# One block of gMLP, SSD and PEER experts on one core: gather rates by stage, and three one-hots made by one comparison

## Chip, cores and metric

The kernel runs on one NeuronCore of a Trainium2 chip. The metric is the device time of one execution in microseconds (us); less is better. Times of the runs of one kernel are given by their median.

## What is computed

The reference is one block over 1024 tokens of width 1024, in fp32. A gMLP branch and an SSD branch (a chunked state-space scan with a causal convolution) are gated, merged, projected and normalised to `x1`. Then comes PEER: 8 heads pick 16 of 16384 experts for every token, that is 128 experts a token.

```python
...
    s1 = jnp.einsum('thd,hkd->thk', q[:, :, 0], sub_k1).astype(jnp.float32)
    s2 = jnp.einsum('thd,hkd->thk', q[:, :, 1], sub_k2).astype(jnp.float32)
    v1, i1 = lax.top_k(s1, PEER_TOPK)
    v2, i2 = lax.top_k(s2, PEER_TOPK)
    cand = (v1[..., :, None] + v2[..., None, :]).reshape(T, PEER_HEADS, PEER_TOPK * PEER_TOPK)
...
    gates = jax.nn.softmax(best, axis=-1)
...
        u = u_tab[eb]
        act = jax.nn.gelu(jnp.einsum('tkd,td->tk', u, xb).astype(jnp.float32))
        return jnp.einsum('tk,tkd->td', (gb * act).astype(x.dtype), v_tab[eb])
...
```

The block's output is the layer norm of `ALPHA * x1`, the PEER sum and a gated projection of `p`.

## The kernel before

**Groups.** The tokens are worked on in three groups (GROUPS): two blocks of 128, three blocks, three blocks. `front(gi)` runs a group through its stages: the gmlp stage (gates of the branch, its mixing and output product), the SSD stage, the merge (`ya`, lines 538 to 551), the query stage (w_o, normalisation, w_q, top 16, and `ple`), and for the last group the gates stage and the dense stage. Products in fp32 are made of three passes over rounded halves (`mm3`, lines 155 to 157); each weight is split into `whi` (line 149, ScalarE) and `wlo` (line 150, VectorE).

**Two ways for the experts.** For the first two groups (5 blocks) the expert rows are gathered. `experts_u` gathers a row of the u table for each of 128 experts of 128 tokens (line 837, an indirect DMA of 128 rows of 4 KB, issued by GpSimd) and multiplies it with `x1` on VectorE with a running sum (line 856). `experts_v` gathers rows of the v table, four at a time, and adds them up on TensorE with diagonal weights (line 898, tile `pacc`): 8 products in the program for a group of four rows, 16 records in the profile. In all these are 5 x 256 = 1280 gathers. The rows go through a ring of 12 buffers.

For the last group the experts are computed densely. `dense_scores` makes the products of all tokens with a part of the u table ahead and stores them in DRAM (`s`). `dense_gates` makes, token by token, a 128x128 matrix of gates as a product of two one-hot matrices: `o1` compares a row of numbers 0 to 127 (`iota`) with the first half of the expert's number, `o2` with the second, times the gate. Four tokens share a PSUM tile. Of these four, the first `o1` is made by ScalarE (lines 974 and 975), the other three by VectorE (line 977); all four `o2` by VectorE (line 979); line 981 multiplies. `dense` then runs through the 16384 experts in 16 steps: products with the u table (or a load of `s`), times the gates, and products with the v table into `po`.

**The order of the work.** Gathers run beside the fronts of the second and third group. Each `yield` of `front` names a cost; a gather costs 1.47. After each yield the loop at the end of `block_kernel` lets as many gathers follow as the cost times `SIDE[phase[0]]` pays for. `phase[0]` is 0 in the gmlp stage, 1 in SSD stage and merge, 2 in the query stage, 3 in the gates stage, 4 in the dense stage. What is left after the last front runs alone. The scheduler keeps that order but for the priorities that are written into the code.

Of the kernel before, what the change touches and what calls it, by code (L numbers as in the profile page):

```python
# [8 lines left out]
F32 = mybir.dt.float32  # L9
# [4 lines left out]
AF = mybir.ActivationFunctionType  # L14
OP = mybir.AluOpType
# [9 lines left out]
TC, GI = 32, 4  # L25
# [3 lines left out]
TOPK = 16  # L29
OFF = [sum(TOPK // (a + 1) for a in range(n)) for n in range(TOPK + 1)]  # L30
PAIRS = HEADS * TOPK
O1_ACT = 1
LAG = 6
QLAG = 4
TOGETHER = 2000
# [7 lines left out]
AHEAD_G = 40  # L43
LEAD = 50
UNIT = 5.35
SIDE = (0.82, 0.78, 0.80, 0.66, 0.78)
ALPHA = 2 ** 0.25
EPS = 1e-5

# [32 lines left out]
def block_kernel(ctx, tc, a, out):  # L82
    nc = tc.nc
    V, A, PE, DMA, POOL = nc.vector, nc.scalar, nc.tensor, nc.sync, nc.gpsimd
# [112 lines left out]
    ps, ps_es, phase, tk_, selects = {}, [None], [0], [None], []  # L197
# [20 lines left out]
    def front(gi):  # L218
# [24 lines left out]
        with tc.tile_pool(name="ga", bufs=1, side=side_) as ga, \  # L243
# [75 lines left out]
            for g4 in range(0, 8, 4):  # L319
# [3 lines left out]
                for g in range(g4, g4 + 4):  # L323
                    V.scalar_tensor_tensor(add[:, g], pr[:, g - g4], gmb[:, g:g + 1], add[:, g],
                                           op0=OP.mult, op1=OP.add)
# [11 lines left out]
            for g in range(8):  # L337
# [4 lines left out]
                for c in range(NB):  # L342
# [5 lines left out]
                                       op0=OP.mult, op1=OP.add)  # L348
# [29 lines left out]
        with tc.tile_pool(name="sa", bufs=1, side=side_) as sa, tc.tile_pool(name="sb", bufs=2, side=side_) as sb:  # L378
# [141 lines left out]
            for n in range(3):  # L520
                pgs.append(channel_major(a["w_g"][8 + n], xh, xl))
                yield unit
                c = next(tail, None)
# [5 lines left out]
            V.reciprocal(rrow, rrow)  # L529


        mp_es = ExitStack()
        mp = mp_es.enter_context(tc.tile_pool(name="mp", bufs=1, side=other))
        mh = mp.tile([128, 8, T], F32R, name="mh")
# [117 lines left out]
        tk_es.close()  # L652
        phase[0] = 3
        yield from merge((take(ahead, AHEAD[1]), AHEAD[1] * unit), (dense_gates(gi, NB, pst), 38 * NB))
        yield from ahead
        phase[0] = 4
# [297 lines left out]
    def dense_gates(gi, NB, pst):  # L954
        with tc.tile_pool(name="da", bufs=1) as da, tc.tile_pool(name="db", bufs=3) as db:
            iota = da.tile([128, 128], F32, name="iota")
            POOL.iota(iota, pattern=[[1, 128]], base=0, channel_multiplier=0,
                      allow_small_or_imprecise_dtypes=True)
            T = NB * 128
            sT = da.tile([128, 3, T], F32, name="sT")  # L960
            for c in range(NB):
                DMA.dma_start(sT[:, :, c * 128:c * 128 + 128], sel_t[gi, c])

            g_d[gi] = dram.tile([T // TC, 128, 128 * TC], F32, name=f"g_{gi}")
            for c in range(T // TC):
                gt = db.tile([128, 128, TC], F32, name="gt", bufs=2)
                for n4 in range(0, TC, 4):
                    p = pst.tile([128, 4, 128], F32, name="mt", tag="mt")
                    for i in range(4):
                        n = c * TC + n4 + i  # L970
                        o1 = db.tile([128, 128], F32, name="o1")
                        if i < O1_ACT:

                            A.activation(o1, iota, AF.Abs, scale=-1.0, bias=sT[:, 0, n:n + 1])
                            A.activation(o1, o1, AF.Relu, scale=-1.0, bias=1.0)
                        else:
                            V.tensor_scalar(o1, iota, sT[:, 0, n:n + 1], None, op0=OP.is_equal)
                        o2 = db.tile([128, 128], F32, name="o2")
                        V.tensor_scalar(o2, iota, sT[:, 1, n:n + 1], sT[:, 2, n:n + 1],  # L979
                                        op0=OP.is_equal, op1=OP.mult)  # L980
                        PE.matmul(p[:, i, :], lhsT=o1, rhs=o2, start=True, stop=True)  # L981
                    A.copy(gt[:, :, n4:n4 + 4].rearrange("p i t -> p t i"), p)
                    yield 1.2
                gf = gt.rearrange("p i t -> p (i t)")
                for b in range(0, 128 * TC, 2048):
                    DMA.dma_start(g_d[gi][c, :, b:b + 2048], gf[:, b:b + 2048])
# [76 lines left out]
    for gi in range(NG):  # L1063
        owed = 0.0
        for cost in front(gi):
            owed += cost * SIDE[phase[0]]
            if not gate_t:
                owed = 0.0
            while side and owed > 0:
                step = next(side[0], None)  # L1070
                if step is None:
                    side.pop(0)
                else:
                    owed -= step
        if GROUPS[gi][1] == "gather":
            selects += [select(gi, c) for c in range(GROUPS[gi][0])]
            side += [experts([(gi, c, r0 + c * 128) for c in range(GROUPS[gi][0])])]
        r0 += GROUPS[gi][0] * 128
# [79 lines left out]
```

## Time and profile before

| | before |
|---|---|
| median of 3 runs | 3757.99 us (3755.95 to 3758.19) |
| the profiled execution | 3754.28 us |
| its span | 3752.6 us |
| TensorE busy | 3439.9 us (92%) |
| VectorE busy | 2935.7 us (78%) |
| ScalarE busy | 1754.2 us (47%) |
| GpSimd busy | 1569.2 us (42%) |
| DMA | 1183.88 MB, mean 315 GB/s |

Busy shares are means over the whole span; the stages have different limits, so a table by stage says more. TensorE's busy time holds some waiting, since its products overlap. The stages are, in us from the span's start: first group to 497; second group 497 to 709 (gmlp), to 1067 (SSD), to 1134 (merge), to 1293 (query); third group to 1543, 1925, 1996, 2320; gates stage to 2616; dense stage 2664 to 3674; then the tail.

### The profile page before, as it was taken

The page shows a single profiled execution, that of the slowest core. Times are in us where ns is not written, and L with a number is a line of the kernel's source. Part 1 is how long each engine was busy: PE and PEld are TensorE (multiplying, and loading weights), DVE is VectorE, ACT ScalarE, POOL GpSimd, SP SyncE. Part 2 cuts the span into 40 slices and gives each one's busy share as a digit, 9 for nine tenths or more (in the row PEclk, how much of TensorE's full clock was granted, in tenths as well). Part 3 has the DMA queues.
Part 4 walks back from the last instruction along what each step waited for, and adds up shares of the span by engine and source line. Part 5 has one row for each costly group of instructions (what it writes and reads, how often), then busy time and mean ns, then how long its engine had stood idle before and what let it go on. Part 6 is the DMA issues. An engine that isn't in the chain of part 4 may idle for free. (4 is left out here: it accounts for less than half of the span.)

```text
span 3752.6 us, 59429 instructions
## 1 busy us (share of the span) xinstructions
PE 3439.9 (92%) x21390; PEld 2939.4 (78%) x21390; DVE 2935.7 (78%) x6823; ACT 1754.2 (47%) x2671; POOL 1569.2 (42%) x1310
## 2 busy tenths in 40 slices
PE   9899996999998988999987989889989999999995
PEld 8888896888887977888777878777768878778771
DVE  6677898898987989894698999997676676676652
ACT  6888443475752333475742334675333323233220
POOL 0000004744455444543455455334455455455544
PEclk9999998999999999999999999999999999999997
DMA  6444647989899787989899899899999999999987
GB/s 212 160 164 160 229 174 249 389 308 356 311 369 391 288 305 285 358 308 323 295 326 337 302 337 371 329 335 370 349 378 379 363 360 370 357 365 395 367 313 283
DMA packets 405703, 1183.88 MB, mean 315 GB/s; under 512 B 40736, under 2 KB 135968, under 8 KB 402336
## 3 DMA queue, kind: packets, MB, share of 16 engines
q0 software_dynamic: 187488, 682.71, 48.5%
q1 hardware_dynamic: 217200, 494.76, 36.8%
q8 instruction: 168, 2.75, 0.3%
q10 hardware_dynamic: 720, 2.62, 0.2%
q14 instruction: 127, 1.04, 0.1%
HBM read 1121.01 MB, written 58.92 MB: 314 GB/s over the span
## 5 line engine op out<-in xcount | busy, mean ns | idle before, releaser
L149 ACT CAST whi<-raw 128x1024 fp32r<-128x1024 f32 (+1 forms) x676 | 700.5, 1041 | 1127.2 <-PE mm L156 582.2
L837 POOL DMA_INDIRECT row<-in_peer_u_dram,idx x640 | 796.3, 1244 | 1004.3 <-PE pacc L898 376.2
L157 PE MATMUL mm<-xh,wlo 128*128 128x384 f32 (+2 forms) x3160 | 1055.3, 335 | 57.4 <-DVE wlo L150 50.5
L150 DVE TENSOR_TENSOR wlo<-raw,whi 128x1024 fp32r<-128x1024 f32 (+1 forms) x676 | 817.1, 1211 | 371.0 <-ACT whi L149 298.7
L155 PE MATMUL mm<-xh,whi 128*128 128x384 f32 (+2 forms) x3160 | 1060.6, 336 | 38.0 <-ACT whi L149 27.2
L156 PE MATMUL mm<-xl,whi 128*128 128x384 f32 (+2 forms) x3160 | 1046.8, 331 | 0.6 <-DVE xl L139 0.6
L837 POOL DMA_INDIRECT row<-in_peer_v_dram,idxT x640 | 758.9, 1186 | 681.9 <-DVE row L856 210.9
L856 DVE SCALAR_TENSOR_TENSOR row<-row,x1b 128x1024 f32<-128x1024 f32 x640 | 773.6, 1217 | 22.9 <-DMA row<-in_peer_u_dram,idx 18.5
L155 PEld LDWEIGHTS mm<-xh,whi 128*128 128x128 f32 (+1 forms) x3160 | 606.9, 192 | 93.4 <-ACT whi L149 51.5
L157 PEld LDWEIGHTS mm<-xh,wlo 128*128 128x128 f32 (+1 forms) x3160 | 606.1, 192 | 78.1 <-DVE wlo L150 60.1
L156 PEld LDWEIGHTS mm<-xl,whi 128*128 128x128 f32 (+1 forms) x3160 | 606.3, 192 | 9.5 <-issue 2.8
L898 PE MATMUL pacc<-row,zw 128*32 128x512 f32 x2560 | 321.3, 621 | 39.2 <-DMA row<-in_peer_v_dram,idxT 39.1
L155 PE MATMUL po<-whi,ewh 128*128 128x512 f32 x768 | 313.9, 409 | 20.1 <-DVE eacc L1051 17.9
L156 PE MATMUL po<-wlo,ewh 128*128 128x512 f32 x768 | 309.4, 403 | 17.1 <-DVE wlo L150 17.0
L157 PE MATMUL po<-whi,ewl 128*128 128x512 f32 x768 | 308.2, 401 | 0.0
L898 PEld LDWEIGHTS pacc<-row,zw 128*32 128x32 f32 x2560 | 68.5, 111 | 193.9 <-issue 140.6
L155 PEld LDWEIGHTS po<-whi,ewh 128*128 128x128 f32 x768 | 147.3, 192 | 86.3 <-DVE eacc L1051 19.9
L156 PEld LDWEIGHTS po<-wlo,ewh 128*128 128x128 f32 x768 | 147.5, 192 | 50.4 <-DVE wlo L150 18.5
L852 POOL DMA_DIRECT2D x1b<-x x5 | 3.0, 606 | 434.2 <-DMA x<-x 434.1
L138 ACT CAST ewh<-ew 128x384 fp32r<-128x384 f32 x128 | 65.6, 513 | 242.4 <-DVE ew L1019 175.3
L157 PEld LDWEIGHTS po<-whi,ewl 128*128 128x128 f32 x768 | 147.4, 192 | 36.1
L981 PE MATMUL mt<-o,o 128*128 128x128 f32 x768 | 148.9, 302 | 15.1 <-DVE o L979 6.0
(275 smaller groups left out, 5609.3 us busy)
## 6 DMA issues: line engine op xcount, KB each, us to landing
raw<-in_peer_uT_dram SPq DMA_DIRECT2D x128, 512.0 KB
raw<-in_peer_vd_dram SPq DMA_DIRECT2D x128, 512.0 KB
raw<-in_w_xbc_dram SPq DMA_DIRECT2D x96, 512.0 KB
raw<-in_w_g_dram SPq DMA_DIRECT2D x48, 512.0 KB
raw<-in_w_z_dram SPq DMA_DIRECT2D x48, 512.0 KB
raw<-in_ssd_w_out_dram SPq DMA_DIRECT2D x48, 512.0 KB
raw<-in_w_q_dram SPq DMA_DIRECT2D x48, 512.0 KB
g<-gt SPq DMA_DIRECT2D x24, 1024.0 KB
```

The source lines that it names most:

```text
L138: A.copy(hi, src)
L149: A.copy(hi, raw)
L150: V.tensor_sub(lo, raw, hi.bitcast(F32))
L155: PE.matmul(p, lhsT=lh, rhs=rh, start=start, stop=False, skip_group_check=skip)
L156: PE.matmul(p, lhsT=lh, rhs=rl, start=False, stop=False, skip_group_check=skip)
L157: PE.matmul(p, lhsT=ll, rhs=rh, start=False, stop=stop, skip_group_check=skip)
L837: g = POOL.indirect_dma_start(out=t, out_offset=None, in_=a[tab], in_offset=bass.IndirectOffsetOnAxis(ap=ix, axis=0))
L852: POOL.dma_start(x1, x1_d[gi, c])
L856: u = V.scalar_tensor_tensor(t, t, 1.0, x1, op0=OP.mult, op1=OP.mult, accum_out=act[:, k:k + 1])
L898: return PE.matmul(pacc[q * 32:q * 32 + 32, h * 512:h * 512 + 512], lhsT=zws[z][:, q, r % 4, :], rhs=ts[q][:, h * 512:h * 512 + 512], star ...
L981: PE.matmul(p[:, i, :], lhsT=o1, rhs=o2, start=True, stop=True)
```

## The change

The table of rates gets other values and a sixth one for the merge, which becomes phase 5. In `dense_gates` the plain one-hots of the last three of four tokens are made by one VectorE comparison of 128x384, `others`, with two buffers of its own; it compares `iota`, repeated three times, with three columns of `sT`, each repeated 128 times. The first token's one-hot stays on ScalarE, in the three buffers of `o1`.

```diff
-O1_ACT = 1
...
-SIDE = (0.82, 0.78, 0.80, 0.66, 0.78)
+SIDE = (0.70, 0.82, 0.68, 0.66, 0.86, 1.1)
...
+        phase[0] = 5
         mp_es = ExitStack()
...
                     p = pst.tile([128, 4, 128], F32, name="mt", tag="mt")
+
+                    n0 = c * TC + n4
+                    first = db.tile([128, 128], F32, name="o1")
+                    A.activation(first, iota, AF.Abs, scale=-1.0, bias=sT[:, 0, n0:n0 + 1])
+                    A.activation(first, first, AF.Relu, scale=-1.0, bias=1.0)
+                    others = db.tile([128, 3, 128], F32, name="o3", bufs=2)
+                    V.tensor_tensor(others, iota[:, None, :].to_broadcast([128, 3, 128]),
+                                    sT[:, 0, n0 + 1:n0 + 4].unsqueeze(2).to_broadcast([128, 3, 128]),
+                                    op=OP.is_equal)
                     for i in range(4):
-                        n = c * TC + n4 + i
-                        o1 = db.tile([128, 128], F32, name="o1")
-                        if i < O1_ACT:
-
-                            A.activation(o1, iota, AF.Abs, scale=-1.0, bias=sT[:, 0, n:n + 1])
-                            A.activation(o1, o1, AF.Relu, scale=-1.0, bias=1.0)
-                        else:
-                            V.tensor_scalar(o1, iota, sT[:, 0, n:n + 1], None, op0=OP.is_equal)
+                        n = n0 + i
+                        o1 = others[:, i - 1] if i else first
                         o2 = db.tile([128, 128], F32, name="o2")
                         V.tensor_scalar(o2, iota, sT[:, 1, n:n + 1], sT[:, 2, n:n + 1],
                                         op0=OP.is_equal, op1=OP.mult)
```

What the rates make of the gathers follows from the code: the sum of a stage's costs times its rate by 1.47 (with what is owed from the yield before).

| stage | sum of costs | rate | gathers | rate after | gathers after |
|---|---|---|---|---|---|
| gmlp, second group (the first yields pay nothing) | 134.8 | 0.82 | 55 | 0.70 | 47 |
| SSD, second group | 265.6 | 0.78 | 141 | 0.82 | 148 |
| merge, second group | 64.2 | 0.78 | 34 | 1.1 | 48 |
| query, second group | 146.7 | 0.80 | 80 | 0.68 | 68 |
| gmlp, third group | 134.8 | 0.82 | 76 | 0.70 | 65 |
| SSD, third group | 265.6 | 0.78 | 141 | 0.82 | 148 |
| merge, third group | 64.2 | 0.78 | 34 | 1.1 | 48 |
| query, third group | 235.0 | 0.80 | 128 | 0.68 | 109 |
| gates | 219.5 | 0.66 | 98 | 0.66 | 98 |
| dense | 849.0 | 0.78 | 451 | 0.86 | 497 |
| left | | | 42 | | 4 |

Three places of the instruction order. Line numbers of the change are one less up to line 530, the same from there to line 968, and three more behind the comparisons.

VectorE, in the merge of the third group, the first of its eight rounds; line 545 opens a round, 547 to 549 are its additions and products, `ml` (139, or 138) its low half, and `row,act` is a gathered u row. Before:

```order
L545 TENSOR_TENSOR sg<-sg,rrow 128x384
L150 TENSOR_TENSOR wlo<-raw,whi 128x1024
L547 TENSOR_TENSOR ya<-ya,mm 128x384
L856 SCALAR_TENSOR_TENSOR row,act<-row,x1b 128x1024
L548 TENSOR_TENSOR ya<-ya,sg 128x384
L856 SCALAR_TENSOR_TENSOR row,act<-row,x1b 128x1024
L549 TENSOR_TENSOR ya<-ya,m0t 128x384
L856 SCALAR_TENSOR_TENSOR row,act<-row,x1b 128x1024
L139 TENSOR_TENSOR ml<-ya,mh 128x384
L856 SCALAR_TENSOR_TENSOR row,act<-row,x1b 128x1024
```

With the change:

```order
L545 TENSOR_TENSOR sg<-sg,rrow 128x384
L547 TENSOR_TENSOR ya<-ya,mm 128x384
L149 TENSOR_TENSOR wlo<-raw,whi 128x1024
L548 TENSOR_TENSOR ya<-ya,sg 128x384
L856 SCALAR_TENSOR_TENSOR row,act<-row,x1b 128x1024
L549 TENSOR_TENSOR ya<-ya,m0t 128x384
L856 SCALAR_TENSOR_TENSOR row,act<-row,x1b 128x1024
L138 TENSOR_TENSOR ml<-ya,mh 128x384
L856 SCALAR_TENSOR_TENSOR row,act<-row,x1b 128x1024 x4
```

Six u rows stand in the round in place of four. From line 545's first row of this merge to the next stage's first row (line 577) there are 37 u rows before and 51 with the change; from there to the gates 71 before and 56 with the change. In the gmlp stages (from line 312 to the first convolution, line 392) there are 59 and 37 before, 55 and 34 with the change.

TensorE, at the end of the program; `po` is the dense stage's output, `pacc` the sum of gathered v rows, x8 a group of four. Before:

```order
L157 MATMUL po<-whi,ewl 128x512
L155 MATMUL po<-whi,ewh 128x512
L156 MATMUL po<-wlo,ewh 128x512
L157 MATMUL po<-whi,ewl 128x512
L898 MATMUL pacc<-row,zw_139 32x512 x32
L898 MATMUL pacc<-row,zw_138 32x512 x32
L898 MATMUL pacc<-row,zw_139 32x512 x32
```

With the change:

```order
L156 MATMUL po<-whi,ewl 128x512
L154 MATMUL po<-whi,ewh 128x512
L155 MATMUL po<-wlo,ewh 128x512
L156 MATMUL po<-whi,ewl 128x512
L898 MATMUL pacc<-row,zw_139 32x512 x16
```

Twelve groups stand behind the last dense product before, two with the change; the other ten have moved in among the dense products.

VectorE, in the gates stage; `o_..` are the one-hots (977 the plain ones and 979 those with the gate; 975 and 982 with the change). Before:

```order
L979 TENSOR_SCALAR o_25100<-iota,sT 128x128
L856 SCALAR_TENSOR_TENSOR row,act<-row,x1b 128x1024
L150 TENSOR_TENSOR wlo<-raw,whi 128x1024
L977 TENSOR_SCALAR o_25103<-iota,sT 128x128
L979 TENSOR_SCALAR o_25105<-iota,sT 128x128
L977 TENSOR_SCALAR o_25108<-iota,sT 128x128
L979 TENSOR_SCALAR o_25110<-iota,sT 128x128
L977 TENSOR_SCALAR o_25113<-iota,sT 128x128
L979 TENSOR_SCALAR o_25115<-iota,sT 128x128
```

With the change:

```order
L975 TENSOR_TENSOR o_25113<-iota,sT 128x384
L982 TENSOR_SCALAR o_25115<-iota,sT 128x128
L982 TENSOR_SCALAR o_25118<-iota,sT 128x128
L982 TENSOR_SCALAR o_25121<-iota,sT 128x128
L982 TENSOR_SCALAR o_25124<-iota,sT 128x128
```

Seven comparisons for four tokens have become five (between them stand rows of other work).

## Rows read from the trace of the kernel before

**Rows 1.** Table of engines by stage, the columns in its first line.

```profile
core 0: us, PE busy (x) PEld busy (x) DVE busy (x) ACT busy (x) POOL busy (x), PEclk, DMA share, GB/s
497.00:709.00 212.00, 180.26 (x1132) 172.49 (x1131) 198.07 (x506) 83.60 (x108) 87.50 (x62) 0.93 0.73 265
709.00:1067.00 358.00, 345.62 (x2272) 304.14 (x2270) 317.47 (x625) 244.32 (x392) 175.96 (x146) 0.99 0.89 331
1067.00:1134.00 67.00, 63.69 (x365) 58.27 (x366) 55.58 (x93) 23.06 (x31) 38.62 (x32) 0.97 1.00 382
1134.00:1293.00 159.00, 147.80 (x1005) 128.47 (x1005) 137.63 (x476) 50.85 (x81) 77.39 (x64) 0.97 0.91 345
1293.00:1543.00 250.00, 219.18 (x1410) 190.39 (x1413) 228.65 (x674) 93.28 (x125) 120.03 (x94) 0.94 0.84 306
1543.00:1925.00 382.00, 363.80 (x2435) 305.90 (x2427) 280.79 (x513) 245.71 (x393) 178.46 (x152) 0.99 0.88 315
1925.00:1996.00 71.00, 61.74 (x313) 58.41 (x314) 68.88 (x111) 21.08 (x29) 38.62 (x32) 0.93 0.99 368
1996.00:2320.00 324.00, 289.35 (x1862) 259.00 (x1864) 304.64 (x996) 113.21 (x154) 155.11 (x126) 0.96 0.90 330
2320.00:2616.00 296.00, 265.82 (x1643) 219.25 (x1636) 267.79 (x847) 196.57 (x345) 122.82 (x108) 0.97 0.92 343
2664.00:3674.00 1010.00, 972.77 (x4962) 762.75 (x4964) 672.85 (x1039) 306.09 (x407) 520.32 (x439) 0.98 0.97 364
```

**Rows 2.** The same table for steps inside the dense stage.

```profile
2708.00:2777.00 69.00, 69.00 (x370) 58.12 (x367) 52.46 (x84) 26.02 (x34) 42.82 (x37) 1.00 1.02 396
3359.00:3505.00 146.00, 146.00 (x781) 119.94 (x780) 102.06 (x153) 47.33 (x62) 84.19 (x69) 1.00 1.01 388
3505.00:3558.00 53.00, 47.16 (x219) 33.60 (x218) 36.60 (x56) 14.04 (x20) 27.21 (x22) 0.94 1.00 367
3631.00:3674.00 43.00, 43.00 (x221) 28.88 (x224) 16.25 (x26) 8.85 (x11) 16.34 (x17) 1.00 0.74 259
```

**Rows 3.** Timeline of the end: start, duration, engine, line, idle time before.

```profile
3641.50 1.92 PE L898 MATMUL pacc<-row,zw 128*32 128x512 f32 x16
3643.36 0.50 PE L155 MATMUL po<-whi,ewh 128*128 128x512 f32 x1
...
3672.62 0.39 PE L157 MATMUL po<-whi,ewl 128*128 128x512 f32 x1
...
3683.49 1.23 DVE L1057 TENSOR_TENSOR eacc<-eacc,row 128x1024 f32<-128x1024 f32 x1
...
3731.78 0.94 POOL L837 DMA_INDIRECT row<-in_peer_v_dram,idxT  x1 [0.31 <-issue]
...
3738.09 2.96 PE L898 MATMUL pacc<-row,zw 128*32 128x512 f32 x16 [2.44 <-DMA row<-in_peer_v_dram,idxT]
...
3741.10 1.22 DVE L802 TENSOR_TENSOR x1b<-x1b,pacc 128x1024 f32<-128x1024 f32 x1 [43.87 <-PE pacc L898]
```

**Rows 4.** The page's first line and its row of the gathers' queue.

```profile
span 3752.6 us, 59429 instructions
...
q0 software_dynamic: 187488, 682.71, 48.5%
```

**Rows 5.** Groups by line and shape: busy us, mean ns of one, idle before.

```profile
L856 DVE SCALAR_TENSOR_TENSOR row<-row,x1b 128x1024 f32<-128x1024 f32 x640 | 773.6, 1217 | 22.9 <-DMA row<-in_peer_u_dram,idx 18.5 <-issue 3.4
...
L979 DVE TENSOR_SCALAR o<-iota,sT 128x128 f32<-128x128 f32 x384 | 131.9, 358 | 0.7 <-PE mm L157 0.2 <-PE mt L981 0.2
...
L977 DVE TENSOR_SCALAR o<-iota,sT 128x128 f32<-128x128 f32 x288 | 84.2, 293 | 18.6 <-PE mt L981 10.5 <-PE mm L156 3.8 <-PE mm L155 2.1
...
L1019 DVE TENSOR_TENSOR ew<-ew,gte 128x384 f32<-128x384 f32 x128 | 71.2, 562 | 84.0 <-DMA ew<-s 66.0 <-ACT ew L1017 9.2 <-DMA gte<-g 8.4
...
L856 DVE DVE_READ_ACCUMULATOR row<-row,x1b 128x1 f32 x640 | 51.7, 81 | 0.0
...
L450 DVE TENSOR_TENSOR xdd<-mt,dtd 128x384 f32<-128x384 f32 x32 | 17.6, 549 | 3.7 <-PE mt L446 2.9 <-issue 0.8
```

## Prediction

> **What bounds the kernel now.** I read the table by stage first [rows 1]: it cuts the span at the instructions that only one stage has. The reader is to see that no engine bounds all of it. The gmlp stages (497 to 709, 1293 to 1543) and the query stage of the last group (1996 to 2320) are VectorE's: it is busy 198.07 of 212, 228.65 of 250 and 304.64 of 324 us, TensorE and the DMA engines less. The two merges (1067 to 1134, 1925 to 1996) have DMA shares of 1.00 and 0.99; in the second VectorE is full too (68.88 of 71). The SSD stages are TensorE's (345.62 of 358, 363.80 of 382) with VectorE and DMA below. In the gates stage (2320 to 2616) VectorE has 267.79 of 296, TensorE 265.82, the DMA share is 0.92. The dense stage (2664 to 3674) has TensorE at 972.77 of 1010 and a DMA share of 0.97.
>
> Inside the dense stage [rows 2] there are two kinds of step. Where the products with the u table are computed beside it, TensorE is busy all of 146 us and the DMA share is 1.01; where they are loaded (3505 to 3558), TensorE is idle for 6 of 53 us and the DMA share is 1.00. Only the last step has DMA to spare: 0.74 over 43 us.
>
> Last come the tail's instructions [rows 3]. The last product of the dense stage begins at 3672.62; 12 groups of gathered rows follow it (the order shows them), and TensorE waits for each pair of groups to land. The last gather is issued at 3731.78, its group starts at 3738.09, the closing additions at 3741.10, and the span ends at 3752.6 [rows 4].
>
> **The price of one gather.** It costs what the stage is short of. On VectorE a u row takes 1217 ns, and 81 for the accumulator [rows 5]: 1.30 us; a v row almost nothing. On TensorE four v rows take 1.86 us (from 3641.50 to 3643.36 [rows 3]), a u row nothing. On the DMA engines a gather is 0.524 MB; the gathers' queue q0 holds 48.5% of 16 engines' span for 682.71 MB [rows 4], so 0.485 x 3752.6 x 0.524 / 682.7 = 1.40 us.
>
> **The change part by part.** The numbers of gathers by stage are those of the table with the diff: cost times rate by 1.47.
>
> Gmlp stages: 8 and 11 gathers fewer. If all were u rows, VectorE would give back 10.4 and 14.3 us; the rows that the order shows on VectorE there are only some 4 fewer in each. I take -6 for each, ends 0 and -12.
>
> SSD stages: 7 gathers more each. TensorE bounds them, half are v rows: 3.5 / 4 x 1.86 = 1.6 us; I take +2 each, ends 0 and 7 x 1.40 = +10.
>
> Merges: 14 gathers more each. The first has no DMA left: 14 x 1.40 = 20 us, less what slips into the next stage; I take +15. In the second the order puts 14 more u rows on VectorE, 14 x 1.30 = 18 us, on a full engine: +18. Ends +5 and +20. What is queued behind these rows on VectorE is the merge's own additions and the weights' low halves, so TensorE waits for them.
>
> Query stages: 12 and 19 fewer. In the first, TensorE is at 147.80 of 159 and gives back v rows, VectorE u rows: -7. In the second VectorE is the bound and the order shows 15 u rows fewer: 15 x 1.30 = 19.5; I take -17. Ends 0 and -25.
>
> Gates stage: the rate stays. 288 comparisons of 128x128 at 293 ns [rows 5] become 96 of 128x384. No comparison of that form is in the trace. The nearest rows are the broadcast multiplication of two operands of 128x384 (549 ns) and the plain one (562 ns); I take 555. Upper end: three of the old ones, 879 ns, no gain. Saved on VectorE: 96 x (879 - 555) = 31 us. The four other comparisons of each four tokens stay (358 ns each), and so do ScalarE's two operations for the first token. VectorE would fall to 237 us, under the DMA engines' 0.92 x 296 = 272, which are late next. So of 31 us I take -18, ends -27 and 0.
>
> One rule speaks against this part. The Trainium skill (VectorE: DVE Perf Modes, section Mode 2×_2P — use both read ports for one tensor) has an fp32 operation with one tensor at two elements a cycle and one with two tensors at one. With that page's fixed term of about 150 cycles, an estimate from it is 223 ns for an old comparison and 556 for the new, 11 us saved instead of 31. The row's 293 ns does not agree with it: the same page's one element a cycle would be 290.
>
> Dense stage: the rate rises from 0.78 to 0.86, 451 gathers become 497. Its lower end is TensorE alone: in its order 12 groups behind the last dense product become 2, so 10 x 1.86 = 18.6 us come into the stage. Its upper end is the DMA queue alone: 46 x 0.524 MB at the stage's own 364 GB/s = 66 us. The loaded steps and the first ones are at their DMA limit, the computed pairs at both limits, the last step has room for 8 gathers. I take +40, near the middle.
>
> The Trainium skill (DMA: Bandwidth & Descriptors, section Where 436 GB/s comes from) states some 358 GB/s of HBM for one core as what binds such transfers; by it the upper end, 46 x 0.524 / 0.358 = 67 us, would be the price. The rows do not bear out that limit, 396 GB/s over 69 us and 388 over 146 [rows 2], but they leave little above.
>
> Tail: from 3673.0 to 3752.6 it is 79.6 us now. With two groups left, the last gathers are issued about when the last dense product runs. Then stand 6.3 us from issue to product (3731.78 to 3738.09), 3.0 of product and 11.5 of closing: 21 us. VectorE closes the dense blocks at the same time (until 3684.72 [rows 3]), which may push it by up to 5. I take 25, so -54; ends -50 and -58.
>
> Nothing is taken for POOL: it issues the same 1280 gathers, and in no stage is it busy over 58%.
>
> Sum: -12 + 4 + 33 - 24 - 18 + 40 - 54 = -31. The profiled execution took 3754.3 us (span 3752.6, 1.7 around it): 3723. It stands 3.7 us under the median of the runs shown, so the median I forecast is 3727, and the rivals below have the same 3.7 in them.
>
> **The rivals.**
>
> One: TensorE alone bounds the dense stage (+19), and the gates stage gives -27. For it: TensorE idles only 37 us of 1010, and windows of 396 GB/s exist. Against it: the loaded step's DMA share of 1.00. Time: 3727 - 21 - 9 = 3697.
>
> Two: the wide comparison is no cheaper than three narrow ones, or the gates stage was not VectorE's. Then -18 falls away: 3745. For it: TensorE and VectorE are 2 us apart there. Against it: the two-operand rows of the same size.
>
> The Trainium skill's rule on two operands (VectorE: DVE Perf Modes, same section) lies on this side: 11 of 31 us left makes -6 of -18, an estimate of 3739.
>
> Three: in dense stage and merges each gather pays at the stage's rate, 0.524 / 0.364 = 1.44 us: 66 and 2 x 20 instead of 40 and 33, so 3727 + 33 = 3760, no change. What the tail gave is spent before it. The limit of the Trainium skill's DMA page (DMA: Bandwidth & Descriptors, same section) would be this case.
>
> Four, slower: the DMA engines are the bound wherever their share is 0.9 or more. Then rival three's prices hold, and taking VectorE's work out of the gates stage (0.92) gives nothing, of the query stages (0.91, 0.90) only half: 3760 + 18 + 12 = 3790. It decides from the point at which the dense stage grows by over 60 us while the gates stage keeps its 296. Against it: 396 GB/s beside stages at 330 to 345.
>
> That the change does not do what it says is unlikely: the order shows the moved rows in merges and tail.
>
> **How the numbers follow.** Forecast 0.50, with a range of its own of 3710 to 3745; rival one 0.14, two 0.10, three 0.14, four 0.12. A measurement of this kernel can tell some 0.2% (7.5 us) from no change: faster 0.50 + 0.14 + 0.10 = 0.74, same 0.14, slower 0.12. The range goes from just under rival one to just over rival three, 3693 to 3764, and leaves out rival four and the outer half of rival one, under 0.2.
>
> **What would show it.** Right: a tail of 21 to 30 us behind the last dense product; the 96 comparisons at 540 to 580 ns and a gates stage of 270 to 285 us; merges of 80 to 90 us; a last query stage near 307; a dense stage of 1035 to 1060. Wrong: a dense stage over 1070, or a gates stage that keeps 296 with VectorE under 240 busy (rivals three and four); comparisons of 700 ns or more (rival two); merges that stay under 72, which would say that DMA had room.

## The result and the profile after

The changed kernel takes 3716.8 us (median of 4 runs, 3707.43 to 3720.9), the kernel before beside it 3758.09 us. The ratio is 0.9886, 95% interval 0.9869 to 0.9904: about 41 us faster, where 3727 was forecast in a range of 3693 to 3764. The profiled execution took 3720.9 us (span 3719.2), 33.4 us of span less than the one of before.

The table of engines by stage of the changed kernel, its columns as in [rows 1]; the two merges, the last query stage and the dense stage:

```profile
1079.00:1155.00 76.00, 68.71 (x393) 58.42 (x393) 61.82 (x105) 21.91 (x29) 49.12 (x40) 0.96 1.03 406
...
1939.00:2019.00 80.00, 60.35 (x289) 56.84 (x288) 76.22 (x126) 18.57 (x25) 53.05 (x40) 0.87 1.00 378
2019.00:2332.00 313.00, 288.82 (x1880) 260.70 (x1878) 298.41 (x986) 115.46 (x160) 143.24 (x111) 0.97 0.88 323
...
2646.00:3697.00 1051.00, 1000.80 (x5132) 769.73 (x5134) 676.14 (x1044) 305.48 (x406) 551.00 (x484) 0.97 0.99 372
```

Against [rows 1]: the merges are longer and full of transfers (GpSimd's instructions went from 32 to 40 in each), the last query stage is shorter, the dense stage is longer and its DMA share went from 0.97 to 0.99.

The wide comparison of the gates stage, from the groups by line and shape:

```profile
L975 DVE TENSOR_TENSOR o<-iota,sT 128x384 f32<-128x384 f32 x96 | 52.7, 549 | 0.0
```

The record of a wide comparison lasts 549 ns where those of three narrow ones last 3 x 293 [rows 5]. That looks like 96 x (879 - 549) = 32 us less of VectorE, but the records of neighbours overlap. From VectorE's timelines, before and with the change (start, length, what; a length behind x2 or x3 is of all of them):

```profile
2399.05 1.22 DVE L856 SCALAR_TENSOR_TENSOR row<-row,x1b 128x1024 f32<-128x1024 f32 x1
2400.19 0.08 DVE L856 DVE_READ_ACCUMULATOR row<-row,x1b 128x1 f32 x1
2400.21 0.29 DVE L977 TENSOR_SCALAR o<-iota,sT 128x128 f32<-128x128 f32 x1
2400.41 0.65 DVE L979 TENSOR_SCALAR o<-iota,sT 128x128 f32<-128x128 f32 x2
2400.98 0.28 DVE L977 TENSOR_SCALAR o<-iota,sT 128x128 f32<-128x128 f32 x1
```

```profile
2402.49 0.56 DVE L975 TENSOR_TENSOR o<-iota,sT 128x384 f32<-128x384 f32 x1
2402.96 0.94 DVE L982 TENSOR_SCALAR o<-iota,sT 128x128 f32<-128x128 f32 x3
```

What follows a narrow comparison starts 0.20 us after it, and 0.47 us after a wide one (medians over the stage: 197 and 469 ns). By that, 96 x (3 x 197 - 469) = 12 us are saved. The whole gates stage in the table of engines, before and with the change:

```profile
2330.00:2664.00 334.00, 297.09 (x1792) 249.13 (x1791) 281.06 (x859) 207.42 (x361) 129.16 (x116) 0.96 0.92 342
```

```profile
2341.00:2646.00 305.00, 276.90 (x1790) 237.43 (x1789) 265.83 (x665) 199.40 (x357) 136.67 (x118) 0.98 0.99 375
```

VectorE's busy time, which counts an overlap once, falls by 15 us (281.06 to 265.83).

The end of the span, from the timeline of TensorE:

```profile
3696.54 0.40 PE L156 MATMUL po<-whi,ewl 128*128 128x512 f32 x1
3696.87 1.92 PE L898 MATMUL pacc<-row,zw 128*32 128x512 f32 x16
3702.78 3.55 PE L898 MATMUL pacc<-row,zw 128*32 128x512 f32 x16 [3.99 <-DMA row<-in_peer_v_dram,idxT]
```

Two groups stand behind the last dense product, the second waits 4 us for its rows, and 16 us later the span ends: 22.3 us of tail where there were 79.6 [rows 3].

To compare stages exactly I cut every profile at the same instructions: the last score product of a group (line 623), the last product with `gh`, the first product with the second half of ssd_w_out, the first with `mh`, the first product of one-hots, the first and the last product into `po`. Lengths in us, worked out from the start times in the timelines:

| | first group | gmlp | SSD | merge | query | gmlp | SSD | merge | query | gates | dense | tail | span |
|---|---|---|---|---|---|---|---|---|---|---|---|---|---|
| before | 495.9 | 212.1 | 359.3 | 66.3 | 159.0 | 250.0 | 382.6 | 65.7 | 339.7 | 333.5 | 1008.9 | 79.6 | 3752.6 |
| after | 500.8 | 208.4 | 369.6 | 76.2 | 157.6 | 245.8 | 380.2 | 80.7 | 322.2 | 304.9 | 1050.4 | 22.3 | 3719.2 |
| wide comparison alone | 498.7 | 205.0 | 357.2 | 67.8 | 154.8 | 250.1 | 378.6 | 65.6 | 342.6 | 294.3 | 1001.9 | 80.6 | 3697.2 |
| rates alone | 497.0 | 202.7 | 360.4 | 79.3 | 153.8 | 244.4 | 376.8 | 80.5 | 321.3 | 313.4 | 1046.3 | 22.1 | 3697.9 |
| dense rate alone | 499.6 | 205.4 | 356.4 | 67.6 | 155.2 | 250.1 | 378.2 | 65.6 | 337.8 | 317.0 | 1047.0 | 19.4 | 3699.4 |
| early rates alone | 498.4 | 201.3 | 358.2 | 77.4 | 152.4 | 244.6 | 377.1 | 80.2 | 320.5 | 312.0 | 1015.9 | 89.6 | 3727.5 |
| change again | 497.1 | 209.3 | 365.1 | 77.9 | 155.3 | 243.1 | 379.8 | 82.6 | 323.9 | 308.1 | 1049.8 | 20.4 | 3712.4 |
| low merge rate | 497.7 | 208.3 | 365.5 | 68.0 | 149.3 | 247.9 | 374.3 | 70.9 | 329.2 | 313.9 | 1077.3 | 31.1 | 3733.5 |
| half the products | 498.9 | 208.3 | 364.6 | 77.3 | 157.4 | 246.8 | 380.0 | 80.5 | 323.0 | 306.8 | 1018.6 | 22.3 | 3684.5 |
| half the bytes | 497.6 | 209.4 | 362.5 | 77.0 | 155.4 | 246.4 | 379.9 | 80.8 | 323.2 | 302.8 | 1017.4 | 22.6 | 3674.8 |
| change beside | 497.0 | 208.8 | 366.0 | 77.8 | 151.1 | 246.5 | 381.5 | 82.3 | 324.0 | 307.4 | 1055.9 | 20.7 | 3719.1 |
| SSD 0.92 | 499.5 | 209.4 | 373.7 | 75.3 | 155.4 | 242.1 | 401.7 | 82.6 | 311.7 | 308.3 | 1039.3 | 21.0 | 3720.0 |
| SSD 1.0 | 501.3 | 209.5 | 387.5 | 76.3 | 155.5 | 242.2 | 426.3 | 74.9 | 310.1 | 312.9 | 1002.9 | 21.0 | 3720.3 |
| SSD 0.92, low merge | 494.6 | 208.7 | 370.2 | 66.8 | 148.6 | 245.5 | 400.1 | 68.8 | 327.8 | 314.1 | 1061.9 | 22.0 | 3729.2 |

The second to fifth stage are the second group's, the sixth to ninth the third's. The first group has no gathers, and its 495 to 501 us show how far equal work differs between profiles.

The gain is made in two places: the tail gives 57.3 us and the dense stage takes 41.5 of them, and the gates stage gives 28.6. The stages between the first group and the gates change by +6 us in sum.

### The profile page after: what moved, and what is told of

It reads as the page before. It is cut to its first block, busy times and chain, and to the rows that moved or that the text cites. A ratio compares the mean times of both kernels' runs of the same rounds, so it can differ in the third digit from the quotient of the medians.

```text
span 3719.2 us, 59232 instructions
## 1 busy us (share of the span) xinstructions
PE 3426.3 (92%) x21390; PEld 2938.2 (79%) x21390; DVE 2921.4 (79%) x6631; ACT 1739.5 (47%) x2666; POOL 1566.7 (42%) x1310
## 3 DMA queue, kind: packets, MB, share of 16 engines
q14 instruction: 126, 1.03, 0.1%
## 4 chain that ended last, share of the span: by engine, by line
PE 56%; DVE 22%; DMA 9%; ACT 6%; issue 4%; another core or an unknown queue 1%; SPq 0%; POOL 0%; POOLq 0%; DVEq 0%; ACTq 0%
PE mm L154 12%; PE mm L156 11%; PE mm L155 11%; PE pacc L898 5%; DVE wlo L149 5%; DVE row L856 5%; PE po L154 4%; PE po L155 4%; PE po L156 4%; DMA ew<-s 3%; PE mt L984 2%; ACT whi L148 1%; DMA row<-in_peer_v_dram,idxT 1%; PE mt L479 1%
## 5 line engine op out<-in xcount | busy, mean ns | idle before, releaser
L898 PE MATMUL pacc<-row,zw 128*32 128x512 f32 x2560 | 313.7, 608 | 13.7 <-DMA row<-in_peer_v_dram,idxT 13.7
L137 ACT CAST ewh<-ew 128x384 fp32r<-128x384 f32 x128 | 65.5, 513 | 242.2 <-DVE ew L1022 170.2
L156 PEld LDWEIGHTS po<-whi,ewl 128*128 128x128 f32 x768 | 148.6, 193 | 36.3
L154 PE MATMUL mm<-whi,xh 128*128 128x256 f32 x512 | 147.5, 288 | 10.2 <-ACT whi L148 9.3
```

Of the source, the lines that this page charges most:

```text
L137: A.copy(hi, src)
L154: PE.matmul(p, lhsT=lh, rhs=rh, start=start, stop=False, skip_group_check=skip)
L156: PE.matmul(p, lhsT=ll, rhs=rh, start=False, stop=stop, skip_group_check=skip)
L898: return PE.matmul(pacc[q * 32:q * 32 + 32, h * 512:h * 512 + 512], lhsT=zws[z][:, q, r % 4, :], rhs=ts[q][:, h * 512:h * 512 + 512], star ...
```

## The experiments

**The parts of the change, each alone.** These four ran on a chip on which the kernel before takes 3722.75 us (16 runs), so the ratios count and not the times, and the stages are compared among the four.

The comparison, with the old rates:

```diff
-                            V.tensor_scalar(o1, iota, sT[:, 0, n:n + 1], None, op0=OP.is_equal)
...
+                    V.tensor_tensor(others, iota[:, None, :].to_broadcast([128, 3, 128]),
```

> The wide comparison alone, with the rates of before. Theory A (the gates stage was bound by VectorE, the DMA engines close behind): the 96 wide comparisons take about 550 ns, the gates stage falls from 334 us to some 306 (first product of one-hots to first dense product), the time by 20 to 28 us to 3730 to 3738. Theory B (all of the gain is the shorter tail, the comparisons lay beside other work): no change, 3758 within 7. Theory C (all of the gain is the comparison, the rates only move time about): 3717.

Measured: 3700.85 us, ratio 0.9941 (0.9919 to 0.9962), 22 us faster. The gates stage takes 294.3 us, where the three runs beside it with the narrow comparison have 312.0 to 317.0. The stages before it are within 5 us of those of the run with the dense rate alone, which has the same rates there. Its window in the table of engines, and that of the run with the dense rate alone, which has the narrow comparison:

```profile
2320.00:2615.00 295.00, 271.52 (x1775) 236.62 (x1772) 261.16 (x658) 198.21 (x356) 131.98 (x114) 0.99 0.99 382
```

```profile
2316.00:2633.00 317.00, 288.16 (x1789) 243.32 (x1788) 278.16 (x857) 207.09 (x361) 129.79 (x116) 0.97 0.97 363
```

With 192 comparisons fewer on VectorE (x857 and x658 are its instructions in the windows) the same work goes through in 22 us less, and now the DMA share stands at 0.99 with 382 GB/s. VectorE's busy time falls by 17 us, less than the stage does, so the cost of the comparison need not be the whole of it. The edit does a second thing: before, the four one-hots `o1` of a tile shared three buffers; now the first has three to itself, and the other three stand in two buffers of their own. The waits of ScalarE for a free buffer, in the same two windows, narrow and then wide (us in all, times, longest):

```profile
ACT o L974 <- PE mt L981: 15.3, 17, 2.1
```

```profile
ACT o L971 <- PE mt L983: 1.9, 4, 0.8
```

No run has the buffers without the wide comparison, so how the 22 us divide between VectorE's time and the buffers is open. Theories B and C both fall: the comparison is neither nothing nor all.

The rates alone:

```diff
-SIDE = (0.82, 0.78, 0.80, 0.66, 0.78)
+SIDE = (0.70, 0.82, 0.68, 0.66, 0.86, 1.1)
```

> The six rates alone, with the narrow comparisons. Theory A: the tail of 79.6 us becomes 22, the dense stage grows by about 41, the earlier stages together change by less than 6: 8 to 18 us faster, 3740 to 3750, and the gates stage keeps about 334 us. Theory B: the whole gain, 3717. Theory C: no change.

Measured: 3697.98 us, ratio 0.9930 (0.9908 to 0.9952), 25 us faster, somewhat more than the 8 to 18 expected. The tail of 22.1 us is as expected, and the gates stage keeps this chip's length with the narrow comparison (313.4 us; the expected 334 was the other chip's). The stages from the second group's gmlp to the last query stage sum to 1819.2 us, against 1816.3 and 1821.7 of the two runs that keep the early rates. The two parts together, 0.6% and 0.7%, make the change's 1.1% within the intervals.

The dense stage's rate alone:

```diff
-SIDE = (0.82, 0.78, 0.80, 0.66, 0.78)
+SIDE = (0.82, 0.78, 0.80, 0.66, 0.86)
```

> Only the dense stage's rate goes from 0.78 to 0.86 (451 gathers become 493, none is left). Theory A (a gather moved from tail to dense stage costs there some 0.9 us, between TensorE's price and that of the DMA engines): dense stage 1009 to about 1047, tail 79.6 to 20 to 24, 14 to 22 us faster. If TensorE alone bounded the dense stage (0.46 us a gather): about 37 us faster. If the DMA engines alone did (1.44 us): about 60 us into the stage, no gain.

Measured: 3701.19 us, ratio 0.9943 (0.9926 to 0.9960), 21.6 us faster. The dense stage takes 1047.0 us against 1001.9 in the run that keeps its rate: 45.1 / 42 = 1.07 us a gather, between TensorE's 0.46 and the 1.44 of the DMA engines. The two runs with the new early rates give (1046.3 - 1015.9) / 46 = 0.66 for the same step of the rate; there is one profile of each. The tail takes 19.4 against 80.6. Most of what the rates bring is in this one number, 21.6 of 25 us.

The early rates alone:

```diff
-SIDE = (0.82, 0.78, 0.80, 0.66, 0.78)
+SIDE = (0.70, 0.82, 0.68, 0.66, 0.78, 1.1)
```

> Only the rates of the stages before the gates change (50 gathers are left for the tail in place of 42). Theory A (what the gmlp and query stages give back is spent in the merges and the SSD stages): the stages up to the gates change by less than 8 us in sum, the tail grows by 8 gathers at about 1.45 us: 3762 to 3772. If the stages bound by VectorE gave more than the merges take: the stages up to the gates shorten by 15 us or more, 3750 or less.

Measured: 3734.54 us, ratio 1.0034 (1.0018 to 1.0051), 12 us slower. The stages before the gates sum to 1811.7 us against 1816.3 and 1821.7 us of the two runs with the old early rates. The tail is 89.6 against 80.6 in the run with the comparison alone. The dense stage, at the same rate, takes 1015.9 against 1001.9, which no theory had: 13.6 us of it stand in its first step, and why is open. As theory A had it, the early rates give nothing by themselves.

**What bounds the dense stage.** The changed kernel again, beside the three runs that follow:

> The changed kernel once more, so that the runs beside it have its stages on the same chip. About 0.988 of the kernel before; dense stage about 1045 us, merges 77 and 80 us.

Measured: 3712.18 us, ratio 0.9874 (0.9850 to 0.9897); dense stage 1049.8, merges 77.9 and 82.6 us.

Half of TensorE's work for the gathered rows there:

```diff
+            half = phase[0] == 4 and 0 < r < QR - 1
...
                 for h, q in ((0, 2), (0, 1), (0, 0), (1, 3), (1, 2), (1, 1), (1, 0)):
+                    if h and half:
+                        continue
```

> Of the gathered v rows' products in the dense stage the second half of the columns is left out (but for the first and last group of a part), so that TensorE has about 0.93 us less in some 60 groups, 55 us; the gathers move as many bytes as in the changed kernel. If TensorE bounds the dense stage: it shortens by 45 us or more. If the DMA engines do: by less than 10. Theory A (both limits are near, the loaded steps are DMA's): by 10 to 30.

Half of the gathers' bytes there:

```diff
-        g = POOL.indirect_dma_start(out=t, out_offset=None, in_=a[tab],
+        g = POOL.indirect_dma_start(out=t[:, :w], out_offset=None, in_=a[tab].rearrange("r (h w) -> (r h) w", w=w),
...
-                ts.append(gather("peer_v", idxT_t[gi, c][:, n:n + 1]))
+                ts.append(gather("peer_v", idxT_t[gi, c][:, n:n + 1], 512 if half else 1024))
```

> In the dense stage each gather moves rows of 512 numbers in place of 1024 (the rows of the tables are read as two rows each; the products are as many as before and read the first half twice; a u row's product on VectorE is over 512). TensorE's work is that of the changed kernel, the gathers' bytes there are about half. If TensorE alone bounds the dense stage: it shortens by less than 15 us. If the DMA engines do: down to TensorE's own time, 60 us or more. Theory A: by 40 to 70, most of it in the steps that load the products.

The dense stage in the table of engines: of the changed kernel again, with half the products, with half the bytes.

```profile
2642.00:3692.00 1050.00, 997.20 (x5130) 767.00 (x5132) 677.09 (x1044) 305.50 (x406) 544.46 (x484) 0.97 0.99 372
```

```profile
2643.00:3662.00 1019.00, 951.69 (x4649) 754.64 (x4647) 673.20 (x1044) 303.75 (x406) 569.58 (x484) 0.96 1.01 383
```

```profile
2634.00:3652.00 1018.00, 990.00 (x5130) 763.68 (x5128) 573.04 (x1044) 305.85 (x406) 521.98 (x484) 0.98 0.81 270
```

Measured: 3686.43 us (2 runs) and 3677.54 us (2 runs) against 3712.18. Each leaves out a part of the sums and is of use as a measurement only. The first is 26 us faster, within theory A's 10 to 30; the second is 35 us faster and misses its 40 to 70. The stage is 31 and 32 us shorter. In the second the u rows' products on VectorE are halved too (677.09 to 573.04 us of busy time), which is not told apart from the bytes.

As a whole the stage looks as if it had two floors at the same height, 1018 us. The steps say otherwise. Cut at each step's first product into `po`, the six steps beside which products with the u table are loaded, the nine beside which they are computed, and the last step, which has neither, take in us:

| | loaded | computed | last |
|---|---|---|---|
| before | 280.7 | 688.0 | 40.1 |
| after | 303.1 | 705.3 | 42.2 |
| change again | 303.1 | 704.7 | 42.2 |
| half the products | 306.7 | 673.1 | 38.7 |
| half the bytes | 271.3 | 704.2 | 42.2 |

One loaded step and the computed step behind it, of the changed kernel again, with half the products, with half the bytes:

```profile
2764.65:2819.10 54.45, 42.30 (x181) 30.21 (x177) 36.21 (x60) 11.47 (x16) 26.70 (x24) 0.87 1.02 375
2819.10:2896.41 77.31, 77.31 (x417) 62.26 (x416) 53.61 (x81) 23.08 (x30) 43.18 (x37) 1.00 1.01 392
```

```profile
2763.11:2820.65 57.54, 40.66 (x164) 30.33 (x161) 36.44 (x60) 11.82 (x17) 26.83 (x25) 0.82 1.00 360
2820.65:2893.76 73.11, 73.11 (x378) 61.01 (x376) 53.28 (x80) 23.11 (x30) 47.94 (x38) 1.00 1.02 400
```

```profile
2753.21:2798.19 44.98, 40.90 (x180) 29.26 (x177) 29.04 (x59) 11.58 (x16) 24.90 (x23) 0.92 0.92 305
2798.19:2875.50 77.31, 77.31 (x417) 62.26 (x416) 43.16 (x79) 23.11 (x30) 41.29 (x37) 1.00 0.75 249
```

The computed step takes 77.31 us at a DMA share of 1.01 and again at 0.75, so the DMA engines did not bound it. TensorE, busy all the time, did: half the products shorten it to 73.11. The loaded step gets no shorter by half the products, at a share of 1.00, and 9 us shorter by half the bytes: the loaded steps wait for transfers. Of what the change adds to the stage, 17.3 us stand in the computed steps, which issue 29 gathers more (0.6 us each), and 22.4 in the loaded ones, which issue 11 more; 9.1 of the 22.4 are the first step's, which issues no more gathers than before.

**Was the merges' rate of 1.1 worth something?**

```diff
-SIDE = (0.70, 0.82, 0.68, 0.66, 0.86, 1.1)
+SIDE = (0.70, 0.82, 0.68, 0.66, 0.90, 0.82)
```

> The merges' rate falls from 1.1 to 0.82 (36 gathers in each, not 48), the dense stage's rises to 0.90 for it (520, not 497). Theory A (a gather costs about 1 us in a merge and about as much in the dense stage): merges 68 to 70 us, dense stage 20 to 24 us longer, the time within 8 us of the changed kernel. If the merge's rate of 1.1 were a gain of its own (a gather there costs under 0.5 us): 10 us or more slower than the changed kernel.

Measured: 3733.74 us, ratio 0.9935 (0.9913 to 0.9957) against 0.9874 of the changed kernel: some 20 us slower than it. Theory A's "within 8 us" was wrong; the rival's reason (under 0.5 us a gather in a merge) does not hold either. The merges give back 9.9 and 11.7 us as expected (0.8 and 1.0 us a gather), but the dense stage takes 27.5 for 23 gathers (1.2 each) and the tail 10.7 more. The tail's cause is in the timelines of this run; TensorE first, then GpSimd:

```profile
3702.32 3.78 PE L898 MATMUL pacc<-row,zw 128*32 128x512 f32 x32
3718.63 3.64 PE L898 MATMUL pacc<-row,zw 128*32 128x512 f32 x16 [12.53 <-DMA row<-in_peer_v_dram,idxT]
```

```profile
3697.76 0.94 POOL L837 DMA_INDIRECT row<-in_peer_v_dram,idxT  x1 [0.30 <-issue]
3704.50 0.93 POOL L837 DMA_INDIRECT row<-in_peer_v_dram,idxT  x1 [5.80 <-PE pacc L898]
```

Five gathers were left instead of four, and so three groups stand behind the last dense product. The gathers of the third are let go only by the products of an earlier group, after the dense stage's end, and land 12 us later. In the changed kernel the last gathers are issued before that.

**Cheaper places for the gathers.** Three kernels were to beat the change by moving gathers from the dense stage to the SSD stages. The changed kernel beside them:

> The changed kernel, for the three runs beside it: 0.987 to 0.990 of the kernel before; dense stage about 1050 us, SSD stages 365 and 380.

Measured: 3710.08 us, ratio 0.9861 (0.9827 to 0.9894).

```diff
-SIDE = (0.70, 0.82, 0.68, 0.66, 0.86, 1.1)
+SIDE = (0.70, 0.92, 0.68, 0.66, 0.80, 1.1)
```

> The SSD stages' rate goes from 0.82 to 0.92 (166 gathers each, not 148), the dense stage's from 0.86 to 0.80 (462, not 497); the merges keep 1.1. Theory A (a gather in the dense stage costs 0.9 to 1.2 us; in an SSD stage, where TensorE is the bound and the DMA share is 0.89, 0.2 to 0.6): SSD stages 4 to 10 us longer each, dense stage 30 to 40 shorter, 15 to 25 us faster than the changed kernel. If the price were the same everywhere (1.4 us of DMA): no difference.

```diff
-SIDE = (0.70, 0.82, 0.68, 0.66, 0.86, 1.1)
+SIDE = (0.70, 1.0, 0.68, 0.66, 0.75, 1.1)
```

> The same further: 1.0 in the SSD stages (181 gathers each), 0.75 in the dense stage (433). Theory A: the SSD stages' DMA share comes to about 1.0, so the second step costs as much as it gives: within 10 us of the run at 0.92. If TensorE stayed the only bound in the SSD stages: 15 us or more under it.

```diff
-SIDE = (0.70, 0.82, 0.68, 0.66, 0.86, 1.1)
+SIDE = (0.70, 0.92, 0.68, 0.66, 0.84, 0.82)
```

> 0.92 in the SSD stages, 0.82 in the merges (36 gathers each), 0.84 in the dense stage (485), so 23 gathers stand in the dense stage that the run at 0.92 has in the merges. Theory A as corrected by the run with the low merges (0.9 us a gather in a merge, about 0.9 in the dense stage below 0.86): within 8 us of the run at 0.92 and 1.1. If the merges' rate of 1.1 is a gain of its own: 10 us or more slower than that run.

Measured: 3725.42 (ratio 0.9904, 0.9875 to 0.9933), 3720.80 (0.9887, 0.9853 to 0.9922) and 3737.4 us (0.9939, 0.9917 to 0.9961). None beats the change. The profile of the changed kernel beside is the slowest of its four runs, so the lengths that follow are kind to the three. Theory A's price for the SSD stages was wrong: 18 gathers more cost 7.7 us in the second group's and 20.2 in the third's (0.4 and 1.1 a gather), 33 more cost 21.5 and 44.8; and 35 fewer in the dense stage gave 16.6 us, not 30 to 40 (64 fewer gave 53.0). The third group's SSD stage, of the changed kernel beside and of the run at 1.0:

```profile
1547.00:1929.00 382.00, 365.96 (x2457) 307.12 (x2456) 281.91 (x514) 244.88 (x393) 184.99 (x157) 0.99 0.89 322
```

```profile
1572.30:1998.60 426.30, 383.68 (x2422) 317.94 (x2421) 337.25 (x609) 245.18 (x394) 222.94 (x191) 0.94 0.91 332
```

At 1.0 TensorE is busy 90% of the stage where it had 96%, though neither VectorE (79%) nor the DMA share (0.91) is full. So no engine is full there any more. The gathers that came into the stage are u rows: VectorE works on 93 where it had 45, and TensorE's products with v rows are no more than before. TensorE's idle time (42.6 us in place of 16.0) is led by waits for VectorE and ScalarE:

```profile
PE mt L452 <- DVE xdd L449: 11.4, 9, 2.9
PE mm L154 <- ACT whi L148: 10.7, 11, 1.6
```

`xdd` stands in VectorE's queue, which the u rows lengthen. That reading was not tested by a run of its own. The last run is 12 us slower than the first of the three, but their intervals overlap, so a worth of the merges' rate is likely here and not shown. In the two profiles, 9 us apart, the merges give back 8.5 and 13.8 us, the dense stage takes 22.6 more for its 23 gathers, and the third group's query stage 16.1 more (327.8 against 311.7) though the numbers of gathers and of u rows there are nearly the same (57 and 59 u rows). Why is open.

## Why the prediction was right, point by point

The time and the sign came out, 3716.8 measured and 3727 forecast, and so did the mechanism of tail, dense stage and merges. The term of the gates stage owes its size to two errors that worked against each other, which is luck. By the terms of the sum, from the first two rows of the table of stages:

| term | forecast | profile |
|---|---|---|
| gmlp stages | -6, -6 | -3.7, -4.2 |
| SSD stages | +2, +2 | +10.3, -2.4 |
| merges | +15, +18 | +9.9, +15.0 |
| query stages | -7, -17 | -1.4, -17.5 |
| gates stage | -18 | -28.6 |
| dense stage | +40 | +41.5 |
| tail | -54 | -57.3 |
| first group | 0 | +4.9 |
| sum | -31 | -33.5 |

- **Tail and dense stage** held within 4 us each. That the dense stage lies "near the middle" between TensorE's price and that of the DMA engines is explained by the two half runs: the computed steps pay about TensorE's price (17.3 us for 8 groups more, 14.9 by 1.86 us each), the loaded steps pay for transfers. One reading behind it was wrong: "the computed pairs at both limits". Half the bytes left those steps as long as they were.
- **Gates stage.** The length of the wide comparison came out, 549 ns for 555, but the saving on VectorE did not: the prediction multiplied lengths of records that overlap, so its 31 us were 15 in the profile and 17 in the run of the part alone. (For the same reason a u row costs some 1.14 us from start to start and not 1.30.) The step from there, "of 31 us I take -18", was too small: the part alone gave 22 us, the profile 28.6, past the end of -27. So one error made the saving too large and the other took too small a part of it. What the sum did not have is the wait for buffers of `o1`. The limit from the old DMA share, 0.92 of the stage, is about what the profile shows (0.92 x 333.5 = 307, measured 304.9). On the other chip it did not hold as a floor: 0.97 x 317.0 = 307 with the narrow comparison, and 294.3 measured with the wide one, whose transfers went at 382 GB/s and not 363. The Trainium skill's rule against this part (VectorE: DVE Perf Modes, section Mode 2×_2P — use both read ports for one tensor) would have left 11 of 31 us saved, which the prediction put at a gain of 6. VectorE's 15 to 17 us are nearer to that than to 31, and the time of 22 is not; no run here shows the one-operand comparison at two elements a cycle.
- **Merges.** 14 more gathers cost 9.9 and 15.0 us. The lower one is under "14 x 1.40 = 20 us, less what slips": the merge went to 406 GB/s where 382 had been read as all there is. The Trainium skill states a limit of some 358 GB/s (DMA: Bandwidth & Descriptors, section Where 436 GB/s comes from); with 406 GB/s over 76 us this trace does not agree.
- **Early stages.** The forecast was that they cancel, +1 in sum; they came to +6 in the profile, and to 5 to 10 us less in the run with the early rates alone. What single stages got was off by up to 8 us, the SSD stage of the second group most (+10.3; +5.8 and +6.7 in the two repeats). That is little more than the 5 us by which the first group, equal work, differs here.
- **Rival one** (TensorE alone bounds the dense stage) falls by the loaded steps, which half the products left no shorter; **rivals three and four** (each gather pays the DMA's price) by 0.7 to 1.1 us a gather in the dense stage and by its computed steps, which half the bytes left as long as they were; **rival two** by the comparison alone, which was 22 us faster.
- **What would show it.** Tail 22.3 (21 to 30), comparisons of 549 ns (540 to 580), dense stage 1050 (1035 to 1060) and the second merge's 80.7 (80 to 90) came as listed; the first merge's 76.2 is under its range. The windows named for gates and query stage were cut loosely; cut at the same instructions the last query stage lost the 17 us and the gates stage 28.6, more than the 11 to 26 that its 270 to 285 stood for.

## What to carry to other kernels

When two streams share a core, the rate of the one beside the other should leave nothing behind: work in the tail has the whole core waiting for it, and cost 57.3 / 38 = 1.5 us a gather there against 0.7 to 1.1 in the dense stage. But a last group too many behind the main stream costs a whole round of release, issue and landing, some 10 us, so count the groups that stand behind the last instruction. And price a moved item by what each stage is short of, with a look at the queue that it lengthens: in a stage without a full engine an item was not free. Cut a stage into its kinds of step before you say what bounds it: two means over the dense stage hid that some steps were TensorE's and some the DMA engines'. And take an engine's saving from its busy time or from start to start, not from the lengths of overlapping records.

## What was not expected of the hardware

- A computed step of the dense stage took 77.31 us at a DMA share of 1.01 (392 GB/s) and 77.31 us at 0.75 (249 GB/s). A full share there was no bound.
- Over the 76 us of a merge the DMA engines moved 406 GB/s at a share of 1.03; the same stage had 382 GB/s at 1.00 before. A share of 1.00 does not yet say that no more fits.
- The gates stage's DMA rate rose from 363 to 382 GB/s with the wide comparison: nearly the same bytes in 295 us for 317, though the share had been 0.97.
- The kernel before takes 3758 to 3761 us in three of the comparisons and 3722.75 us in the one with the four parts: 1% between chips, as much as the change itself. Of these 36 us some 16 to 22 seem to stand in the gates stage (333.5 us against 312.0 to 317.0 with the narrow comparison). Times were compared by ratios to runs on the same chip.
